# Two places instead of one for the copies of the linear attention's query and key projections

## The chip, the cores and the metric

The kernel runs on one core of one Trainium2 chip. The metric is the device time of one launch in microseconds (us), as the median of several runs. A core has five engines that run their own instruction streams: PE (matrix products; PEld is its loading of weights), DVE (vector), ACT (scalar functions and copies), POOL (a second vector engine) and SP, which here only issues transfers (DMAs). An engine takes its instructions in the order in which they were written; a semaphore makes it wait for another engine or for a DMA.

## The reference

One layer of a hybrid decoder on 16 learned meta tokens and 2048 tokens of width 1024, in float32:

```python
h = layer_norm(concat([meta, x]))
q_s, k_s, v_s, q_g, k_g, v_g, r_g, g_lr = split(h @ w_in + b_in)
o_s = sliding_window_gqa(q_s, k_s, v_s, sinks)        # 8 heads, window 128
log_g = log_sigmoid(g_lr @ w_gate_lr2 + b_gate_lr2) / 16
o_g = chunked_gla(q_g, k_g, v_g, log_g)               # linear attention, 4 heads
o_g = rms_norm(o_g, gla_norm_g) * silu(r_g)
h = layer_norm(ALPHA * h + concat([o_s, o_g]) @ w_out)
h = layer_norm(ALPHA * h + swiglu(h))                 # 1024 -> 2816 -> 1024
return h[16:]
```

The change concerns `q_g` and `k_g`, 256 columns each: four units of 128 columns of the input projection.

## The kernel before

The 2048 tokens are worked in four blocks `s` of 512. The program has three stages.

**First stage** (to about 400 us). Per block, the layer norm (`load_tokens`, 128 tokens at a time: load, normalise, transpose on PE, `tp`, split into a high and a low part `h`), the input projections for the window attention, the window attention itself, and the projections of `q_g` and `k_g`. A projection (`project`) is 24 PE matmuls of 512 columns (line 197, tile `pu`; three products of high and low parts over eight slices of the depth) into one of **two** PSUM buffers (`mm_psum`, `bufs=2`). An ACT instruction then adds the bias, writes the result to SBUF, and by that frees the PSUM buffer for the projection after the next. For `q_g` and `k_g` (`gla_qk`, lines 686 to 693) this copy is line 692, the tile is `gr`, and a DMA (line 693, on SP's queue, for the last block on ACT's) stores it to the scratch tensor `gqk_sc`, from where the second stage loads it. Units 6 to 9 are `gr` 0 to 3, unit 0 is the window's keys, unit 2 its first queries.

The window attention runs in steps of two 128-token blocks: scores (`s`, lines 627 and 628), mask and maximum on DVE, eight exponentials on ACT (line 643), sums, `pr` scaled on POOL (line 652), then a transpose of the meta part (`pmn` on ACT, `tm` on PE, `ptm`), transposes of the rest (`pt`, line 668), the high part `pch` (ACT) and low part `pcl` (DVE) of these, their masked forms `pbh` (DVE, line 672) and `pbl` (POOL, line 673), and the products with the values (`oa`, lines 675 and 680), whose copy `ms` is stored too.

**Second stage** (to about 930 us). Value, gate and output-gate projections, the chunked linear attention (`lp`, `amat`, `op`, `ot`), the output projection (`po`) with its residual (`yo`, line 930), layer norm and transposes (`nt`, line 943). **Third stage**: the feed-forward network, with a fast matrix scheme of seven products instead of eight.

The program names steps in the order of the string `WINDOW_STEPS` (`... V1 G3 S3 G2 G1 V2 ...`, where `G2` is `gla_qk` with `c = 2`), but this is not the order in which an engine gets them. `tile.TileContext(nc, schedule_with_timeline_sim=True)` lays the instructions of each engine out by a planner that follows the readiness of the tiles in a time model; only steps marked `held` keep the written order. A tile's count of places (`bufs`) therefore sets two things: what must wait at run time, and where the planner puts every later instruction. With `bufs=1`, the copy to `gr` can start only when the store of the previous `gr` has read it.

Of the kernel before, what the change touches and what calls it, by code (L numbers as in the profile page):

```python
# [8 lines left out]
F32 = mybir.dt.float32  # L9
# [5 lines left out]
P = 128  # L15
# [108 lines left out]
def body(ctx, tc, t, seq):  # L124
# [150 lines left out]
    with ExitStack() as c1:  # L275
# [3 lines left out]
        wp = c1.enter_context(tc.tile_pool(name="wp", bufs=1))  # L279
# [242 lines left out]
        def project(u, s, h, want_meta=False):  # L522
            w, pt = begun.pop((u, s), None) or (units_ahead.pop((u, s), None) or unit(t["w_u"][u], f"u{u}_{s}", P, None, key=u), mm_psum(f"pu{u}_{s}"))
            terms = lambda a, b: [m for k in range(KT) for m in ((w[:, 0, k, :], a(k)), (w[:, 0, k, :], b(k)), (w[:, 1, k, :], a(k)))]
            c = halves[1] if s == 0 and u < EARLY_UNITS else slice(0, TB)
            last_matmul[:] = [matmuls(pt[:, c], terms(lambda k: at(h, 0, k)[:, c], lambda k: at(h, 1, k)[:, c]), held if s == 0 and u < 2 else lambda i: i)]
            if s == 0 and u in FIRST_UNITS[:-1]:
                ahead(FIRST_UNITS[FIRST_UNITS.index(u) + 1], 0)
            if want_meta:
                metas[u] = w  # L530
            return pt
# [3 lines left out]
        def project_meta(o, u, b):  # L535
            w = metas.pop(u)
            pm = acc_psum(f"pm{u}")[:, : 2 * NM].rearrange("p (a m) -> p a m", m=NM)
            for k in range(KT):
                nc.tensor.matmul(pm, w[:, 0, k, :], hm[:, :, k, :], start=(k == 0), stop=False)
                nc.tensor.matmul(pm[:, 0, :], w[:, 1, k, :], hm[:, 0, k, :], start=False, stop=(k == KT - 1))  # L540
            nc.scalar.activation(o, pm[:, 0, :], AF.Identity, bias=b)
            nc.vector.tensor_tensor(o, o, pm[:, 1, :], op=ALU.add)
# [143 lines left out]
        def gla_qk(s, c, h):  # L686
            u = 6 + c
            pt = project(u, s, h, s == 0 and c >= 2)
            if s == 0 and c >= 2:
                project_meta(kTm[:, c - 2, :], u, bu[:, u : u + 1])  # L690
            raw = wp.tile([P, 512], F32, tag="gr", name=f"gr{s}_{c}", bufs=1)
            nc.scalar.activation(raw, pt, AF.Identity, bias=bu[:, u : u + 1])  # L692
            (nc.scalar if s == NSB - 1 else nc.sync).dma_start(gqk_sc[s * NB : (s + 1) * NB, :, c, :].rearrange("n p q -> p n q"), raw.rearrange("p (n q) -> p n q", q=P))

# [17 lines left out]
        for s in range(NSB):  # L712
            if s == NSB - 2:
                with behind(anchor):
                    tri, head, bvg, gng, eye, lev, w2, brh, brg = gla_constants()
            if s + 1 < NSB:
                hid[s + 1] = hidden(s + 1)
            for what in WINDOW_STEPS.split():
                op, k = what[0], int(what[1])
                if op == "q":  # L720
                    qs[s, k] = swa_q(s, k, hid[s])
                elif op == "S":
                    swa_scores(s, k, {c: qs.get((s, c)) for c in range(4)})
                elif op == "V":
                    swa_values(s, k)
                elif op == "G":
                    gla_qk(s, k, hid[s])
                elif s + 1 < NSB:
                    if op == "L":
                        with behind(ends if (s, k) == (0, 0) else ()):  # L730
                            load_tokens(s + 1, hid[s + 1], k)
                    elif op == "K":
                        (swa_keys, swa_vals)[k](s + 1, hid[s + 1])
                    else:
                        qs[s + 1, k] = swa_q(s + 1, k, hid[s + 1])
            if s == 0:
                with behind(stored_parts[-1:]):
                    for o, x in put_off:
                        nc.sync.dma_start(o, x)
# [105 lines left out]
    wp = c3.enter_context(tc.tile_pool(name="gw", bufs=1, reuse_waits="tile"))  # L845
# [490 lines left out]
    raw, factors = {}, {}  # L1336
# [258 lines left out]
    AFTER, f = {}, None  # L1595
    for what in FIRST_PRODUCTS.split():
        if what[0] == "P":
            f = EARLY[int(what[1])]
# [147 lines left out]
```

## Time and profile before

| | |
|---|---|
| median of 3 runs | 2222.5 us (2222.38 to 2226.02) |
| the profiled execution: its own time | 2216.87 us |
| its span, first to last instruction | 2215.0 us |
| PE busy | 2158.8 us, 97% of the span |
| mean granted PE clock | 0.993 |
| copies to `gr` (line 692) | 16, 687 ns each (median), 57.9 to 378.0 us |
| their stores to `gqk_sc` | 12 by SP, 4 by ACT; 256 KB each, 5.1 us to landing (median; 2.3 to 10.5) |

Time outside the span is 2216.87 - 2215.0 = 1.9 us. PE is busy nearly throughout, so what counts are the intervals in which PE waits, and the clock that it is granted. A group's row in the profile has, after the bar, its busy time, the mean of one instruction, and the idle time just before its instructions with what ended most of it. A row of the timeline has start, length, engine, line, operation, the number of instructions merged, and in brackets the idle time before the first and what ended it. PE's instructions overlap in the pipeline, so lengths of single matmuls are longer than their distance: a 512-column matmul follows another after about 0.23 us, a 128- or 256-column one after 0.12 us.

### The profile page before, as it was taken

To read this page: it belongs to the slowest core of one execution; us is meant where nothing else is said; L and a number is where in the kernel's file an instruction comes from. 1 tells how busy PE (TensorE), PEld (TensorE's weight loads), DVE (VectorE), ACT (ScalarE), POOL (GpSimd) and SP (SyncE) were. 2 spreads that over 40 slices of the span, in tenths; PEclk is the share of its full clock that TensorE was granted. 3 is DMA by queue.
4 is the path that set the end of the run, shared out by engine and by line. 5 is a ranking of instruction groups with operands and counts; after the bars stand their busy time and mean duration, and the time that the engine had idled before them with its cause. 6 is when DMAs were issued, how large, how long until landed. Compare 5 with 4: busy or idle time off the path is not lost.

```text
span 2215.0 us, 31559 instructions
## 1 busy us (share of the span) xinstructions
PE 2158.8 (97%) x11564; PEld 1858.7 (84%) x11564; DVE 1444.7 (65%) x2285; ACT 838.1 (38%) x1477; POOL 1220.2 (55%) x951
## 2 busy tenths in 40 slices
PE   8899999999999999999999999999999999999998
PEld 7788888889999998878888888788888888888886
DVE  6556645466745576368998567766656555876787
ACT  5544644544352443342223223322223242232443
POOL 4656645655634071368776666776666536432433
PEclk9999999999999999999999999999999999999999
DMA  8987773576786787766352318523232299655463
GB/s 296 316 277 252 254 268 127 193 277 226 290 294 225 253 310 244 274 252 219 130 196 103 131 45 286 189 101 109 90 125 81 98 360 330 219 185 177 166 232 124
DMA packets 181918, 460.92 MB, mean 208 GB/s; under 512 B 16978, under 2 KB 65011, under 8 KB 167684
## 3 DMA queue, kind: packets, MB, share of 16 engines
q1 hardware_dynamic: 176804, 452.26, 58.1%
q10 hardware_dynamic: 4960, 6.65, 0.8%
q8 instruction: 92, 1.51, 0.3%
q14 instruction: 62, 0.51, 0.1%
HBM read 306.67 MB, written 152.17 MB: 207 GB/s over the span
## 4 chain that ended last, share of the span: by engine, by line
PE 85%; DMA 4%; DVE 4%; POOL 3%; issue 2%; ACT 2%; SPq 0%; DVEq 0%; POOLq 0%; ACTq 0%
PE t L197 20%; PE d L1377 18%; PE b L197 14%; PE pu L197 13%; PE po L197 6%; PE pv L197 4%; PE lp L1151 2%; PE oa L680 1%; DMA r_t<-t_sc 1%; DMA cb<-n_scT 1%; DMA x<-x 1%; PE s L627 1%; PE s L628 1%; ACT pr L643 1%; PE nt L943 1%
## 5 line engine op out<-in xcount | busy, mean ns | idle before, releaser
L1377 PE MATMUL d<-B,A 128*128 128x512 f32 x1848 | 419.0, 389 | 0.0
L1377 PEld LDWEIGHTS d<-B,A 128*128 128x128 f32 x1848 | 346.9, 188 | 72.0
L197 PE MATMUL t<-h_t,ps 128*128 128x512 f32 x1584 | 367.9, 390 | 3.2 <-DMA ps<-parts_ps 2.4
L197 PEld LDWEIGHTS t<-h_t,ps 128*128 128x128 f32 x1584 | 296.8, 188 | 65.8 <-issue 2.1
L197 PE MATMUL pu<-h,hl_u 128*128 128x512 f32 (+1 forms) x1032 | 249.3, 389 | 7.2 <-ACT gr L692 4.5
L197 PE MATMUL b<-h_b,pa 128*128 128x512 f32 x1032 | 241.9, 390 | 0.3 <-ACT pa L185 0.2
L197 PEld LDWEIGHTS b<-h_b,pa 128*128 128x128 f32 x1032 | 193.7, 188 | 41.3 <-ACT pa L185 0.7
L186 POOL TENSOR_TENSOR pa<-a,pa 128x1024 fp32r<-128x1024 f32 x62 | 160.7, 2591 | 103.8 <-ACT pa L185 103.8
L197 PEld LDWEIGHTS pu<-h,hl_u 128*128 128x128 f32 x1032 | 184.0, 197 | 38.8 <-ACT gr L692 5.1
L197 PE MATMUL po<-hl_o,msh 128*128 128x256 f32 x1024 | 198.3, 289 | 4.8 <-DVE yo L930 3.1
L186 DVE TENSOR_TENSOR A<-rA,A 128x1024 fp32r<-128x1024 f32 (+1 forms) x78 | 117.2, 1527 | 119.7 <-ACT A L185 119.7
L197 PEld LDWEIGHTS po<-hl_o,msh 128*128 128x128 f32 x1024 | 162.1, 191 | 6.6 <-DVE yo L930 4.2
L185 ACT ACTIVATE A<-rA 128x1024 fp32r<-128x1024 f32 (+1 forms) x78 | 78.6, 1042 | 215.2 <-PE d L1377 200.2
L197 PE MATMUL po<-hl_o,msl 128*128 128x256 f32 x512 | 146.3, 286 | 0.0
L1647 DVE TENSOR_TENSOR u<-u,t 128x512 f32<-128x512 f32 x132 | 89.3, 680 | 84.2 <-PE t L197 84.1
L197 PE MATMUL b<-h_b,ps 128*128 128x512 f32 x528 | 126.9, 396 | 2.9 <-ACT h_b L185 2.8
L197 PE MATMUL t<-h_t,pa 128*128 128x512 f32 x528 | 123.8, 390 | 0.0
L1573 POOL TENSOR_TENSOR a<-a,a 128x1024 f32<-128x1024 f32 x42 | 121.2, 2887 | 1.6
L197 PEld LDWEIGHTS b<-h_b,ps 128*128 128x128 f32 x528 | 100.8, 191 | 25.0 <-ACT h_b L185 3.2
L197 PEld LDWEIGHTS t<-h_t,pa 128*128 128x128 f32 x528 | 99.0, 188 | 20.4
L185 ACT ACTIVATE ps<-a 128x1024 fp32r<-128x1024 f32 x63 | 66.7, 1059 | 123.4 <-PE t L197 81.9
L185 ACT ACTIVATE pa<-a 128x1024 fp32r<-128x1024 f32 x62 | 65.8, 1060 | 110.1 <-PE t L197 52.7
(355 smaller groups left out, 4292.0 us busy)
## 6 DMA issues: line engine op xcount, KB each, us to landing
hl_u<-w_u SPq DMA_DIRECT2D x42, 1024.0 KB, 6.7
a<-w_gu SPq DMA_DIRECT2D x84, 512.0 KB, 4.2
rA<-a_sc SPq DMA_DIRECT2D x66, 512.0 KB, 4.6
w<-w_d SPq DMA_DIRECT2D x50, 512.0 KB, 5.5
hl_o<-w_o SPq DMA_DIRECT2D x24, 1024.0 KB, 8.0
hT_sc<-h SPq DMA_DIRECT2D x32, 512.0 KB, 6.0
gh<-hT_sc SPq DMA_DIRECT2D x16, 1024.0 KB, 10.5
w_u<-hl_u SPq DMA_DIRECT2D x14, 1024.0 KB, 8.3
```

The lines of the kernel that those rows point to most:

```text
L185: hold(nc.scalar.activation(hi, src, AF.Copy))
L186: hold((lo_eng or nc.vector).tensor_tensor(lo, src, r32(hi), op=ALU.subtract))
L197: last = hold(nc.tensor.matmul(out, l, r, start=(i == 0), stop=(i == n - 1)))
L627: nc.tensor.matmul(sp[:, :272], q, khh[:, hh, w], start=True, stop=False)
L628: nc.tensor.matmul(sp[:, :272], q, kll[:, hh, w], start=False, stop=True)
L643: nc.scalar.activation(pr[:, n, x, :], pr[:, n, x, :], AF.Exp, bias=nm[:, n, x : x + 1], scale=SLOPES[c0 + x // 2 + 4 * (x % 2)], accum_ou ...
L680: nc.tensor.matmul(oa[:, n], l, m, start=False, stop=(hh == 1 and i == 5))
L943: nc.tensor.transpose(tp[:, n, :], self.ys[n][:, k * P : (k + 1) * P], ident)
L1151: nc.tensor.matmul(o[:, P * j : P * j + P], kl[:, j, :], x[:, :, j, :], start=True, stop=True)
L1377: nc.tensor.matmul(pt, a_[:, a, ca], fb[:, b, cb], start=(p == 0 and j == 0), stop=(p == NP - 1 and j == 2))
L1573: sub = lambda o, x, y: nc.gpsimd.tensor_tensor(o, x, y, op=ALU.subtract)
L1647: nc.vector.tensor_tensor(o[i], x[i], y[i], op=ALU.add)
```

## The change

The tile of the copies of `q_g` and `k_g` gets two places in SBUF:

```diff
@@ -688,7 +688,7 @@
             pt = project(u, s, h, s == 0 and c >= 2)
             if s == 0 and c >= 2:
                 project_meta(kTm[:, c - 2, :], u, bu[:, u : u + 1])
-            raw = wp.tile([P, 512], F32, tag="gr", name=f"gr{s}_{c}", bufs=1)
+            raw = wp.tile([P, 512], F32, tag="gr", name=f"gr{s}_{c}", bufs=2)
             nc.scalar.activation(raw, pt, AF.Identity, bias=bu[:, u : u + 1])
             (nc.scalar if s == NSB - 1 else nc.sync).dma_start(gqk_sc[...], raw...)
```

It takes 2 KB more of each partition in the pool `wp`, and no instruction is added or removed. But the planner now orders much of the program otherwise: from PE's row 149 (near 105 us) to its row 2626 (near 930 us) the rows stand in another order, and the other engines' likewise; behind that only a few rows of the second group of feed-forward products differ. Three places follow; a `+` is a row of the changed kernel, a `-` one of the kernel before; the last number of a name tells tiles of one name apart.

**First place: the first block's key unit 8.** On ACT, in the window attention's first steps; `gr_2` is the copy of unit 8, `h` and `x` belong to the layer norm:

```order
 L185 ACTIVATE h_0_712<-tp_0_1063 128x4x128
 L660 ACTIVATE pmn_0_846<-pr_0_784 128x128
+L692 ACTIVATE gr_2_1413<-pu_0_1362,bu 128x512
 L180 ACTIVATE x_1508<-x_1508,lm_in_1519,lr_in_1517 128x1024
 L185 ACTIVATE h_1_713<-tp_1_1070 128x4x128
```

The copy stood behind the eight exponentials of the second attention step; now it stands ahead of them. On PE, some instructions later, `pu_1_1547` is unit 0 of the next block (it takes the PSUM buffer that `gr_2`'s copy frees), `oa_0` the first step's products with the values:

```order
 L680 MATMUL oa_0_851<-pch_0_1_884,vl 128x256
+L197 MATMUL pu_1_1547<-h_0_712,hl_u_1_1545 128x512
 L680 MATMUL oa_0_851<-pcl_0_1_885,vh 128x256
 L391 MATMUL tp_1_1534<-ident,x_1508 128x128 x4
+L197 MATMUL pu_1_1547<-h_0_712,hl_u_1_1545 128x512 x11
 L680 MATMUL oa_0_851<-pbh_0_1_886,vdh 128x256
 L680 MATMUL oa_0_851<-pbh_0_1_886,vdl 128x256
```

The first twelve of unit 0's 24 matmuls now stand ahead of `oa<-pbh`; before, all of them stood behind the step's last `oa` and four scores. A little later on PE, the second attention step, in the kernel before:

```order
 L668 MATMUL pt_1_1_1215<-ident,pr_1_948 128x128 x4
 L197 MATMUL pu_1_1648<-h_0_712,hl_u_1_1646 128x512 x12
 L197 MATMUL pu_1_1648<-h_1_713,hl_u_1_1646 128x512 x4
 L627 MATMUL s_3_0_1151<-khh,qs_3_942 128x272
 L628 MATMUL s_3_0_1151<-kll,qs_3_942 128x272
 L680 MATMUL oa_1_1187<-pch_1_0_1193,vh 128x256
```

and in the changed one:

```order
 L668 MATMUL pt_1_1_1215<-ident,pr_1_948 128x128 x4
 L627 MATMUL s_2_1_1146<-khh,qs_2_1112 128x272
 L628 MATMUL s_2_1_1146<-kll,qs_2_1112 128x272
 L680 MATMUL oa_1_1187<-pch_1_0_1193,vh 128x256
 L680 MATMUL oa_1_1187<-pch_1_0_1193,vl 128x256
 L680 MATMUL oa_1_1187<-pcl_1_0_1194,vh 128x256
 L680 MATMUL oa_1_1187<-pbh_1_0_1195,vdh 128x256
```

Sixteen matmuls of unit 2 stood between the transposes `pt` and the products that need what is made of them; now two scores stand there, and unit 2 comes behind the products.

**Second place: PE in the second block**, near 205 us; `tm_1_2220` is the transpose of the meta part of that block's second attention step, `pu_2_2540` and `pu_2_2641` are units 0 and 2 of the third block:

```order
 L628 MATMUL s_3_1_2174<-kll,qs_3_1986 128x272
-L661 MATMUL tm_1_2220<-ident,pmn_1_2221 128x128
-L668 MATMUL pt_1_0_2227<-ident,pr_1_1992 128x128 x4
-L197 MATMUL pu_2_2540<-h_0_1766,hl_u_2_2538 128x512
-L197 MATMUL pu_2_2641<-h_0_1766,hl_u_2_2639 128x512
-L675 MATMUL oa_1_2226<-ptm_1_2224,vbd 128x128 x2
-L668 MATMUL pt_1_1_2254<-ident,pr_1_1992 128x128 x4
+L391 MATMUL tp_1_2527<-ident,x_2501 128x128 x4
+L197 MATMUL pu_2_2540<-h_0_1766,hl_u_2_2538 128x512 x11
+L197 MATMUL pu_2_2641<-h_0_1766,hl_u_2_2639 128x512 x10
 L627 MATMUL s_2_0_2180<-khh,qs_2_2151 128x272
```

In the changed kernel `tm` follows two rows below this piece, behind 21 matmuls of the projections; before, it followed the scores at once.

**Third place: PE at the end of the second stage**, near 905 us; `nt_7` is the last group of transposes of the third block's `yo` tiles, `po_1_1` and `po_2_1` are output products of the fourth block:

```order
 L197 MATMUL po_1_1_10306<-hl_o_1_1_10278,msl_9993 128x256
+L943 MATMUL nt_7_10268<-ident,yo_0_9266 128x128
+L943 MATMUL nt_7_10268<-ident,yo_1_9268 128x128
+L943 MATMUL nt_7_10268<-ident,yo_2_9270 128x128
+L943 MATMUL nt_7_10268<-ident,yo_3_9272 128x128
 L197 MATMUL po_1_1_10306<-hl_o_1_1_10278,msh_9992 128x256
-L943 MATMUL nt_5_10252<-ident,yo_0_9266 128x128
-L943 MATMUL nt_5_10252<-ident,yo_1_9268 128x128
-L943 MATMUL nt_5_10252<-ident,yo_2_9270 128x128
-L943 MATMUL nt_5_10252<-ident,yo_3_9272 128x128
 L197 MATMUL po_2_1_10332<-hl_o_1_0_10276,msh_9992 128x256
```

The last transposes stood behind the 24 matmuls of `po_2_1`; now they stand one matmul ahead of its first. The buffer of `yo_0` is the one into which the fourth block's last residual tile is loaded once they are done.

## The prediction

> **What bounds the kernel now.** I read the page first: engines, the chain that ended last, the costliest groups.
>
> ```profile
> PE 2158.8 (97%) x11564; PEld 1858.7 (84%) x11564; DVE 1444.7 (65%) x2285; ACT 838.1 (38%) x1477; POOL 1220.2 (55%) x951
> PE 85%; DMA 4%; DVE 4%; POOL 3%; issue 2%; ACT 2%; SPq 0%; DVEq 0%; POOLq 0%; ACTq 0%
> L197 PE MATMUL pu<-h,hl_u 128*128 128x512 f32 (+1 forms) x1032 | 249.3, 389 | 7.2 <-ACT gr L692 4.5
> ```
>
> PE is the bound, so a change is worth what it takes off PE's idle time or adds to its clock. Line 692 is the largest releaser of idle time that is named for a projection: 4.5 us. Next I read who waits for `gr`, and PE's timeline there.
>
> ```profile
>   PE pu L197: 4.5, 2
>   ACT gr L692: 2.9, 3
> ...
> 58.60 0.74 PE L197 MATMUL pu<-h,hl_u 128*128 128x512 f32 x2 [1.06 <-ACT gr L692]
> ...
> 106.60 0.39 PE L680 MATMUL oa<-pbh,vdh 128*128 128x256 f32 x1 [0.66 <-DVE pbh L672]
> 111.86 6.03 PE L197 MATMUL pu<-h,hl_u 128*128 128x512 f32 x19 [3.41 <-ACT gr L692]
> ```
>
> The 4.5 us are two waits. That at 58.60 lies ahead of the first row that is moved (near 105 us) and stays. The one at 111.86 is 3.41 us: unit 0 needs the PSUM buffer that the copy of unit 8 frees. SP and ACT show why the copy came so late:
>
> ```profile
> 100.61 1.49 SPq L693 DMA_DIRECT2D gqk_sc<-gr  x1
> ...
> 107.36 0.42 ACT L643 ACTIVATE pr<-pr,nm 128x144 f32<-128x144 f32 x1 [0.78 <-DVE nm L639]
> ...
> 111.13 0.67 ACT L692 ACTIVATE gr<-pu,bu 128x512 f32<-128x512 f32 x1
> 114.10 0.31 ACT L660 ACTIVATE pmn<-pr 128x128 f32<-128x128 f32 x1 [2.29 <-POOL pr L652]
> ```
>
> It is queued behind exponentials that run without a gap from 107.36 to 111.13. The planner put it there because the one place was still being stored: the store of the `gr` before was issued by SP at 100.61 only. Two windows behind the wait, and the whole stretch that is reordered:
>
> ```profile
> 112.00:114.00 2.00, 2.00 (x5) 1.61 (x6) 1.76 (x6) 0.00 (x0) 2.00 (x2) 0.50 1.12 365
> 114.00:116.00 2.00, 2.00 (x8) 1.57 (x8) 0.21 (x1) 1.46 (x2) 0.57 (x2) 0.77 1.03 391
> ...
> 100.00:400.00 300.00, 291.04 (x1748) 256.78 (x1746) 171.89 (x548) 151.81 (x416) 167.09 (x143) 0.99 0.69 229
> 400.00:930.00 530.00, 513.09 (x3755) 480.31 (x3755) 312.86 (x678) 219.85 (x480) 241.09 (x401) 1.00 0.74 267
> ```
>
> (Columns: window, its length, PE, PEld, DVE, ACT, POOL busy, granted clock, DMA share, GB/s.) PE idles 8.96 + 16.91 = 25.9 us between 100 and 930 us. That is all that any new order can win there, apart from the clock.
>
> **The change part by part.** No instruction is added, so each term is a wait that goes, comes or moves. I go through the places in time.
>
> *The wait itself:* **-3.41 us**. In the new order the copy stands among ACT's work near 94 us, before the exponentials, and its own PSUM tile was finished before that. Unit 0's first half can then start once `h` is there: its low part is done at 104.49 + 0.68 = 105.17,
>
> ```profile
> 104.49 0.68 DVE L186 TENSOR_TENSOR h<-tp,h 128x512 fp32r<-128x512 f32 x1
> ```
>
> and PE arrives at the first of the twelve at about 105.1, needing only the high part for it. What hides the copy's wait is now 5.6 us of unit 0 (24 matmuls, 0.235 apart: the row of sixteen at 121.38 below, less a last one of 0.39, over 15). Were `h` later, PE would stand on `h` instead. Range: 0 to -3.41.
>
> *The clock behind it:* half speed for 2 us and 0.77 for 2 us cost 2 x 0.50 + 2 x 0.23 = **-1.46 us**, if no idle stretch of that kind remains. [...]
>
> *The 0.66 us for `pbh`* at 106.60 are covered by the eleven matmuls now ahead of it (11 x 0.235 = 2.6): **-0.66**.
>
> *New: the second attention step has lost its cover.* Sixteen projection matmuls (3.74 us) stood between its `pt` and its `oa`. How long the chain takes is in its rows of before:
>
> ```profile
> 119.47 0.60 PE L668 MATMUL pt<-ident,pr 128*128 128x128 f32 x4
> 121.38 3.91 PE L197 MATMUL pu<-h,hl_u 128*128 128x512 f32 x16
> ...
> 121.39 0.69 DVE L186 TENSOR_TENSOR pcl<-pt,pch 128x512 fp32r<-128x512 f32 x1
> 122.00 1.41 DVE L672 TENSOR_TENSOR pbh<-pch,mprev 128x512 fp32r<-128x512 f32 x1
> 122.81 1.75 POOL L673 TENSOR_TENSOR pbl<-pcl,mprev 128x512 fp32r<-128x512 f32 x1
> ```
>
> The first four transposes take four distances of 0.12 and end near 119.95; `pbh` is ready 3.46 us later, `pbl` 4.61. In the new order PE wants `pbh` after 13 short matmuls (13 x 0.12 = 1.6) and `pbl` 0.5 later. So PE waits some 1.9 for the one and 0.6 for the other: **+2.5 us**. Low end 0 (DVE did a step of scores ahead of `pcl` here; without it the chain is some 1 us shorter, and a later PE would hide the rest). High end: the second half's `pbl`, for which POOL needs 1.75 more, waits 0.5 too, and the clock's 1.46 is lost again: 4.5. I take the rows as they stand.
>
> *New: `tm` of that step.* Its `pmn` was ready at 114.41 and PE came later, being held up. Now PE has 24 projection matmuls, nine `oa` and eight scores from 105.1 on, some 8.3 us with the transposes, and stands at `tm` near 113.4. ACT gains one copy there, since `ms` moves behind the exponentials, but unit 0's copy (`kr`) now stands ahead of `pmn`, each about the 0.67 of `gr`; so `pmn` ends near 114.2: **+0.8** (0 to 1.4). POOL, which scales `pr`, is free there.
>
> *Queues that the store is moved past.* SP issues the store of unit 8 earlier, ahead of a load of `x`, two stores of the layer norm and the load of unit 2's weights:
>
> ```profile
> 109.37 1.33 SPq L221 DMA_DIRECT2D hl_u<-w_u x1
> ...
> hl_u<-w_u SPq DMA_DIRECT2D x42, 1024.0 KB, 6.7
> ```
>
> An issue takes 1.3 to 1.5 us here (the rows at 109.37 and 100.61), so these weights land at about 109.4 + 1.5 + 6.7 = 117.6; unit 2 starts near 119: **0**, and the cover is 1.4 us. If it were gone (SP's queue another 3 us late), a wait of 1.6 us would stand there.
>
> *Near 205 us* PE waits for `pmn`, which stood behind a copy that waited for its single place:
>
> ```profile
> 204.30 0.69 ACT L692 ACTIVATE gr<-pu,bu 128x512 f32<-128x512 f32 x1 [0.29 <-DMA gqk_sc<-gr]
> 204.89 0.30 ACT L660 ACTIVATE pmn<-pr 128x128 f32<-128x128 f32 x1
> 205.24 0.33 PE L661 MATMUL tm<-ident,pmn 128*128 128x128 f32 x1 [1.30 <-ACT pmn L660]
> ```
>
> With 21 projection matmuls (4.9 us) ahead of `tm` this goes: **-1.30** (0 to -1.30).
>
> *Near 915 us* PE waits for a residual add that waits for a load into a buffer that the last `nt` frees:
>
> ```profile
> 908.48 0.60 PE L943 MATMUL nt<-ident,yo 128*128 128x128 f32 x4
> ...
> 914.43 0.75 DVE L930 SCALAR_TENSOR_TENSOR yo<-yo,po 128x256 f32<-128x256 f32 x2 [1.36 <-DMA yo<-h_sc]
> 914.90 0.38 PE L197 MATMUL po<-hl_o,msh 128*128 128x256 f32 x1 [2.61 <-DVE yo L930]
> ```
>
> `nt_7` moves ahead of 25 matmuls of 0.12 us, 3.0 us in all, which would cover the 2.61. SP's queue must follow, and more stores stand around that load; I take **-2.0** (0 to -2.61).
>
> *All other waits between 115 and 930 us* are dealt anew: 25.9 - 4.07 - 1.30 - 2.61 = 17.9 us in some thirty waits of under 2 us. The attention chains of the later steps stand no closer in the new order than before, and some that were short have more between `pt` and `oa`. I expect the same total: **0**, with half of it either way, -9 to +9.
>
> Sum: -3.41 - 1.46 - 0.66 + 2.5 + 0.8 - 1.30 - 2.0 + 0 = **-5.5 us**; the profiled execution would go from 2216.87 to 2211.4. The runs' median is 2222.5, 5.6 above that execution, so I set the forecast against the median: 2222.5 - 5.5 = **2217.0 us**. Its own range: without the gains at 205 and 915 us, -2.2; with a third of the other waits gone, -11: 2211.5 to 2220.3.
>
> **The rivals.**
>
> *A new wait takes the old one's place* (no change). The second step's chain waits with 4.5 in place of 2.5, `tm` with 1.4, and the places at 205 and 915 us give nothing: -5.53 + 4.5 + 1.4 = +0.4, 2222.9 us. For it: the cover of 16 matmuls is gone, by the order. [...]
>
> *The new order costs more than the wait* (slower). The mechanism is PE's clock: somewhere in the reordered 800 us, PE stands for about 2.5 us and then runs at half speed. This trace prices it by the worst such place, at 58 to 72 us:
>
> ```profile
> 60.76 1.12 PE L391 MATMUL tp<-ident,x 128*128 128x128 f32 x4 [1.42 <-DVE h L186]
> ...
> 60.00:70.00 10.00, 8.77 (x32) 7.78 (x33) 9.43 (x16) 2.03 (x7) 9.25 (x6) 0.52 0.84 274
> ```
>
> 1.06 + 1.42 us of waiting, then 10 x 0.48 = 4.8 us of clock: 7.3 us. Two such places less the sum above: -5.5 + 14.6 = +9.1, 2231.6 us; it decides from new waits of 10 us on. For it: 2598 lines of difference on PE, from a planner that does not know the clock. Against it: the 2.61 us at 914.90 went without a loss (1.00 in the window 400 to 930).
>
> *The copy moves and PE gains nothing, since the copy is still held up on ACT:* 2222.5. Against it: nothing but PE's own result is waited for in front of it. This is part of the no-change case.
>
> **How the numbers follow.** The forecast has 0.58, no change 0.26, slower 0.16. A measurement of this kernel tells about 0.2%, 4.4 us, from no change; of the forecast's 0.58 I count 0.08 below that. So faster 0.50, same 0.34, slower 0.16. The range reaches from 2209 (0.06 below) to 2227 (0.10 above, most of the slower case); the likeliest case's own is above.
>
> **What would show it.** Right: no wait of `pu` for `gr` after 100 us, clock 1.00 from 105 to 120 us, waits of `oa` on `pbh` and `pbl` near 117 us of 1 to 3 us, no wait for `pmn` above 1 us near 200 us, and no wait for `yo` above 1 us before 930 us; behind 1000 us every wait as before, some 5 us earlier. Wrong: granted clock under 1.00 anywhere between 105 and 930 us, PE idle there above 25.9 us, or a wait of the second step above 4 us.

## The result, and the profile after

| | before | after |
|---|---|---|
| median | 2222.5 us (5 runs, 2217.15 to 2226.02) | **2238.1 us** (5 runs, 2232.41 to 2240.98) |
| ratio, 95% interval | | **1.0073** (1.006 to 1.0087): slower |
| profiled execution, its span | 2216.87, 2215.0 us | 2232.41, 2230.5 us |
| mean granted PE clock in it | 0.993 | 0.988 |

The forecast was 2217.0 us, in a range of 2209 to 2227. The change costs 15.6 us.

The page of after, in the rows that answer to those shown of before (engines, the projections' group):

```profile
PE 2166.1 (97%) x11564; PEld 1864.1 (84%) x11564; DVE 1434.8 (64%) x2285; ACT 837.1 (38%) x1477; POOL 1218.8 (55%) x951
L197 PE MATMUL pu<-h,hl_u 128*128 128x512 f32 (+1 forms) x1032 | 248.3, 388 | 7.5 <-ACT h L185 2.9
```

The same instructions keep PE busy 7.3 us longer (2158.8 before), at a mean granted clock of 0.988 in place of 0.993, and PE idles 2230.5 - 2166.1 = 64.4 us in place of 56.2. The largest releaser of the projections is no longer `gr` but `h`.

**The first place came out as forecast.** ACT's and PE's timeline of after:

```profile
94.30 0.69 ACT L692 ACTIVATE gr<-pu,bu 128x512 f32<-128x512 f32 x1 [0.55 <-PE pu L197]
...
105.50 0.40 PE L197 MATMUL pu<-h,hl_u 128*128 128x512 f32 x1
106.21 2.75 PE L197 MATMUL pu<-h,hl_u 128*128 128x512 f32 x11
114.40 0.33 PE L661 MATMUL tm<-ident,pmn 128*128 128x128 f32 x1 [0.60 <-ACT pmn L660]
117.16 0.39 PE L680 MATMUL oa<-pcl,vh 128*128 128x256 f32 x1 [0.32 <-DVE pcl L186]
```

and its window there (columns as below):

```profile
110.00:120.00 10.00, 8.68 (x54) 7.15 (x53) 7.39 (x31) 4.69 (x14) 4.38 (x4) 1.00 1.05 330
```

The copy of unit 8 is done at 95.0, unit 0 starts at 105.50 without a wait for `gr`, the clock is 1.00, and the second attention step waits a little on `tm` and `oa`.

**The loss lies in the second stage.** Windows of before and of after by stage (window, its length, then PE, PEld, DVE, ACT, POOL busy with their counts, granted clock, DMA share, GB/s). Before:

```profile
400.00:510.00 110.00, 103.36 (x693) 91.25 (x693) 64.60 (x148) 51.54 (x121) 65.94 (x107) 1.00 0.69 248
510.00:685.00 175.00, 175.00 (x1272) 165.06 (x1271) 100.71 (x213) 77.19 (x158) 87.23 (x149) 1.00 0.80 290
685.00:940.00 255.00, 244.73 (x1869) 233.66 (x1868) 154.81 (x337) 95.91 (x207) 90.72 (x150) 1.00 0.70 253
```

After:

```profile
100.00:400.00 300.00, 292.54 (x1743) 257.78 (x1741) 166.90 (x542) 152.47 (x415) 166.53 (x141) 0.99 0.70 229
400.00:510.00 110.00, 105.48 (x702) 94.45 (x702) 68.19 (x154) 51.46 (x124) 67.46 (x109) 0.97 0.70 252
510.00:685.00 175.00, 168.43 (x1174) 157.59 (x1173) 95.02 (x203) 76.30 (x155) 85.93 (x144) 0.97 0.72 260
685.00:940.00 255.00, 243.72 (x1847) 232.50 (x1846) 146.48 (x326) 88.71 (x201) 87.09 (x149) 0.99 0.74 268
```

Before, PE does not idle at all from 510 to 685 us: 175.00 of 175.00, at full clock. After, it idles 6.57 us there, has a clock of 0.97, and gets 1174 matmuls done in place of 1272. The waits that PE has between 510 and 935 us say of what kind this is (releaser: us in total, times, the longest). Before, 9.9 us in all, of which the longest are:

```profile
PE po L197 <- DVE yo L930: 3.1, 2, 2.6
PE lp L1151 <- DVE amat L1153: 1.8, 1, 1.8
PE po L197 <- DMA hl_o<-w_o: 1.5, 1, 1.5
PE ot L1190 <- ACT ogn L1187: 1.2, 1, 1.2
```

After, 17.7 us, among them:

```profile
PE lp L1151 <- DVE xq L1146: 4.4, 5, 1.5
PE pu L197 <- DMA hl_u<-w_u: 2.9, 2, 2.1
PE po L197 <- ACT p L1655: 2.3, 1, 2.3
...
PE nt L943 <- ACT yo L180: 1.5, 1, 1.5
PE kt L1163 <- DVE e L1130: 1.3, 1, 1.3
```

Nearly every wait is another one. None has to do with `gr`.

Since no instruction is added, the two programs can be compared point by point: where both orders have issued the same set of PE instructions, how much later does the next one start than before? (One profiled execution each; in the first 60 us two executions of the same order differ by up to 3.4 us and have come together to 0.8 by 71.)

| start before, us | 71.5 | 115.9 | 131.6 | 508.7 | 621.9 | 683.2 | 914.9 | 2112.7 |
|---|---|---|---|---|---|---|---|---|
| after, us later | 0.0 | -5.7 | -3.3 | 0.1 | 8.1 | 12.0 | 15.3 | 15.9 |

The gain is there (-5.7, of which the second attention step takes 2.4 back), is lost between 131 and 508 us, and from 508 to 915 us another 15 us go. Between 131 and 508 us it is the clock that takes the gain: from 130 to 510 us PE idles 10.7 us, in place of 11.5 before, but the granted clock is 0.51 from 202 to 209 us, 0.58 from 400 to 404 and 0.57 from 461 to 465, where before has 1.00.

### The profile page after: what moved, and what is told of

The parts are those of the page before. It is cut to its first block, busy times and chain, and to the rows that moved or that the text cites. A ratio compares the mean times of both kernels' runs of the same rounds, so it can differ in the third digit from the quotient of the medians.

```text
span 2230.5 us, 31549 instructions
## 1 busy us (share of the span) xinstructions
PE 2166.1 (97%) x11564; PEld 1864.1 (84%) x11564; DVE 1434.8 (64%) x2285; ACT 837.1 (38%) x1477; POOL 1218.8 (55%) x951
## 4 chain that ended last, share of the span: by engine, by line
PE 86%; DVE 5%; DMA 4%; POOL 2%; issue 2%; ACT 1%; SPq 0%; DVEq 0%; ACTq 0%; POOLq 0%
PE t L197 21%; PE d L1377 17%; PE b L197 15%; PE pu L197 12%; PE po L197 7%; PE pv L197 4%; PE oa L680 2%; PE lp L1151 2%; PE s L627 1%; DMA hl_u<-w_u 1%; PE s L628 1%; PE nt L943 1%; PE oa L675 1%; DMA cb<-n_scT 1%; PE pt L668 1%
## 5 line engine op out<-in xcount | busy, mean ns | idle before, releaser
L185 ACT ACTIVATE ps<-a 128x1024 fp32r<-128x1024 f32 x63 | 66.6, 1058 | 115.9 <-PE t L197 74.8
L186 DVE TENSOR_TENSOR ps<-a,ps 128x1024 fp32r<-128x1024 f32 x42 | 75.9, 1807 | 50.5 <-ACT ps L185 50.5
```

The source lines that it names most:

```text
L185: hold(nc.scalar.activation(hi, src, AF.Copy))
L186: hold((lo_eng or nc.vector).tensor_tensor(lo, src, r32(hi), op=ALU.subtract))
```

## The experiments

Two things changed at once, the place and the order. My theory was now that the whole loss is the redrawn order. The rivals: that the second place costs by itself, that the loss begins with the moved copy and is carried on, and, in the words of the prediction, that it is the clock.

To part them, the order is held by hand. The program is planned once with one place and once with two, each plan is read as a list for each engine, and a third build is made in which each instruction is tied behind its predecessor in the wanted list, without a semaphore. The list may follow one plan up to a certain PE instruction and the other from there on:

```python
for k in order:
    e = engine[k]
    if e in last:
        tc.add_manual_dep(written[k], written[last[e]].name, ...NoSync..., reason="order")
    last[e] = k
```

`PLACES` is what stands as `bufs` in line 691; `PARTS` lists (plan with so many places, up to which PE instruction). All runs are timed beside runs of the kernel before on the same chip.

### Place and order apart

The order of before with two places:

```diff
+PLACES = 2
+PARTS = [(1, None)]
```

> Two places as in the change, but every instruction on every engine held to the order of the kernel before. Theory (the redrawn order is the whole loss, a second place by itself costs nothing): 2222.5 us, within 0.2% of before, half-clock stretches as before (33.6 us in sum). Rival (the second place itself costs, by its address, its semaphores or what its earlier stores collide with): 2238 us, a ratio near 1.007.

Measured: 2220.85 us, ratio 0.9999 (0.9987 to 1.001). The new order with one place:

```diff
+PLACES = 1
+PARTS = [(2, None)]
```

> One place as before, but every instruction held to the order that the change gets. Theory (order is the loss): 2238 us or more; the copy of unit 8 now waits near 94 us on ScalarE for the one place, which the store issued near 100 us frees, so 3 to 8 us more in the first stage: 2238 to 2246. Rival (the second place itself costs): back to about 2222 to 2230 us.

Measured: 2248.79 us, 1.0124 (1.0108 to 1.014). ACT's and PE's rows of this run show the wait, which is longer than I had put it:

```profile
105.31 0.69 ACT L692 ACTIVATE gr<-pu,bu 128x512 f32<-128x512 f32 x1 [12.71 <-DMA gqk_sc<-gr]
...
107.83 1.22 PE L675 MATMUL oa<-ptm,vbd 128*128 128x128 f32 x4 [7.23 <-ACT ptm L663]
```

With one place ACT stands 12.71 us on the store, and PE 7.23. So the second place itself costs nothing that can be measured, and the new order needs it; the order is the loss.

### Where the loss is

The old order up to 508 us, then the new one, and the mirror of this:

```diff
+PARTS = [(1, 2707), (2, None)]
```

> Two places, the order of before up to TensorE's instruction 2707 (508 us in both traces), then the order of the change. Theory (the loss lies behind 508 us, where the same instruction starts 0.05 us later than before at 508, 8.1 at 622, 12.0 at 683, 15.2 at 930): 2238 us, ratio about 1.007, and the half-clock stretch near 560 us there again. Rival (the loss begins with the moved copy and is only carried): 2222 us.

Measured: 2233.47 us, 1.0061 (1.0046 to 1.0076).

```diff
+PARTS = [(2, 2707), (1, None)]
```

> Two places, the order of the change up to TensorE's instruction 2707 (508 us), then the order of before: the mirror of the run with the halves the other way round. Theory (the two halves add up; the change as a whole is 1.0073, its second half alone 1.0061, so 0.0012 is left for the first half, most of it a granted clock that is lower by about 10 us of half speed at 202, 400 and 461 us while the waits are 2 us fewer): 2221 to 2226 us, ratio 1.000 to 1.002. Rival (the first half sets up a state, such as buffers or loads that come late, from which the loss behind 508 us follows): over 2230 us.

Measured: 2220.62 us, 0.9999 (0.9989 to 1.0009). Within the intervals the loss is all behind 508 us, and the first half does not set it up. The first of the two runs also shows what the clock has to do with it. Its window from 510 to 685 us, and its longest waits between 510 and 935 us:

```profile
510.00:685.00 175.00, 166.73 (x1191) 155.82 (x1191) 98.55 (x207) 76.82 (x157) 86.43 (x146) 1.00 0.75 266
```

```profile
PE lp L1151 <- DVE xq L1146: 4.4, 5, 1.5
PE pu L197 <- DMA hl_u<-w_u: 2.6, 1, 2.6
PE po L197 <- ACT p L1655: 2.5, 1, 2.5
PE kt L1163 <- DVE e L1130: 2.4, 1, 2.4
PE lp L1159 <- DVE amat L1157: 1.7, 2, 0.9
```

From 510 to 685 us the clock is 1.00 here, as before the change, and yet PE idles 8.27 us; over 510 to 935 us the waits are 20.7 us in place of 9.9. The mean granted clock of its six runs is 0.991, that of the 23 runs of before beside them 0.9915; the five runs of the change have 0.988. An estimate of time at full clock (mean time by mean clock) gives 2202.6 for before, 2215.3 for this run and 2211.0 for the change: here 12.7 us of the 13.5 are waits, in the change about 8 are waits and 7 or 8 clock. The end is nearly the same; why, no run shows. So the loss does not need the clock: the order of the second stage costs 13 us at the clock of before. In the change itself, though, about half of the loss is clock.

Two stretches of the new order alone, 508 to 622 us and from 683 us on:

```diff
+PARTS = [(1, 2707), (2, 3444), (1, None)]
```

> Two places, the order of the change for TensorE's instructions 2707 to 3444 alone (508 to 622 us), the order of before ahead of and behind them. Theory (the loss is a sum of waits, place by place; this stretch lost 5.9 us in the run that went over at 508 us, by five waits for xq and amat of 5.1 us in sum): 2225 to 2227 us, ratio 1.002 to 1.003, and the waits near 557 and 560 us again. Rival (a limit behind them takes such waits up later): 2220 to 2222 us, ratio under 1.001.

Measured: 2227.72 us, 1.0029 (1.0018 to 1.0041), with the waits where they were (1.16 us at 558.58, and PE's row behind it):

```profile
561.45 0.71 PE L1151 MATMUL lp<-xq,e 128*128 128x128 f32 x4 [1.48 <-DVE xq L1146]
```

```diff
+PARTS = [(1, 3832), (2, None)]
```

> Two places, the order of before up to TensorE's instruction 3832 (683 us), then the order of the change. Theory (sum of waits: 9.5 us of the 14 were lost ahead of 683 us, 4 to 6 us behind it, at 798, 896 and 899 us and behind 985 us): 2223 to 2226 us, ratio 1.0015 to 1.0027. Rival (the waits behind 683 us follow from the lateness that the stretch before brought): 2219 to 2221 us, ratio within 0.0005 of 1.

Measured: 2226.62 us, 1.0026 (1.0015 to 1.0037), with 1.53 us before `nt` at 888.37 and this before `po`:

```profile
891.67 0.58 PE L197 MATMUL po<-hl_o,msh 128*128 128x256 f32 x1 [2.86 <-ACT p L1655]
```

The two stretches add up to 0.0055 of the 0.0061; the rest is within the intervals, and the piece between them, 622 to 683 us, was not run alone. Each of the two stretches costs its time whatever comes ahead of it, and nothing behind it gives that back.

### What the removed wait is worth

The new order only through the first place, to 116 us and to 131 us:

```diff
+PARTS = [(2, 508), (1, None)]
```

> Two places, the order of the change for TensorE's first 508 instructions (to unit 0's first half, 110 us), then the order of before. Theory (the wait that the change removes is worth what the first place showed, 4.8 us from 71 to 110 us, and the rest of the redraw is what costs): 2217.5 us, ratio 0.9975 to 0.9985, with no wait of pu for gr over 1 us and no half clock at 111 us. Rival (the gain is given back at the next common wait whatever the order): 2222 us.

Measured: 2219.83 us, 0.9994 (0.9983 to 1.0006): this cannot be told from no change, and the theory's 0.9975 to 0.9985 is missed. This version moves unit 0's first half ahead but keeps the old order behind it, and there PE waits for the scores' maximum (below), with a clock of 0.72 from 120 to 130 us behind it:

```profile
117.12 0.36 PE L627 MATMUL s<-khh,qs 128*128 128x272 f32 x1 [1.66 <-DVE mx L630]
```

```diff
+PARTS = [(2, 601), (1, None)]
```

> Two places, the order of the change up to TensorE's instruction 601 (131 us, behind the second attention step), then the order of before. Theory (the removed wait and its neighbours are a real gain of 3.2 us at that point, which the order of before keeps to the end): 2218 us, ratio 0.998 to 0.999. Rival (the clock or a later wait takes it back, as when the order went back at 116 us, where half speed came 7 us later and for 6.8 us): 2221 to 2222 us, ratio 0.9995 to 1.0005.

Measured: **2217.5 us, 0.9988 (0.998 to 0.9997)**. This version has the second place, the gain at the first place and the old second stage, and it is faster than both kernels, though than the one before by a narrow margin: the interval ends at 0.9997. From 100 to 130 us its clock is 1.00 throughout, and its window from 510 to 685 us has no idle again:

```profile
510.00:685.00 175.00, 175.00 (x1274) 165.32 (x1273) 99.51 (x212) 76.70 (x157) 87.74 (x150) 1.00 0.80 291
```

### Can the waits be taken away one by one?

On the run that goes over to the new order at 508 us, three instructions or groups are moved within their engine's list (engine, first, behind the last, to before):

```diff
+MOVES = [("SP", 294, 295, 287), ("PE", 4517, 4519, 4529), ("DVE", 1201, 1202, 1200)]
```

> As the run that goes over to the order of the change at 508 us (2233.5 us, ratio 1.0061), with three places of its second half mended by hand: the load of unit 12's weights issued ahead of two loads and a store that it stood behind (wait of 2.60 us at 668 us), the two transposes of kt put behind ten matmuls of unit 12 that need nothing new (wait of 2.40 us at 798 us), and the last mixing product on VectorE put ahead of one subtraction (wait of 2.45 us at 899.5 us, 1.1 us of it). Theory (the loss is the sum of waits that the new order happens to have): the three give back 4 to 6 us, 2228 to 2230 us, ratio 1.0035 to 1.0045, and the first two waits are under 0.3 us in the trace. Rival (the loss sits in one limit behind the waits, such as VectorE or the loads, so a wait that is taken away comes back at the next place): 2232 to 2235 us, ratio 1.0055 to 1.007.

Measured: 2235.82 us, 1.0068 (1.0054 to 1.0082), so my theory failed here and the rival held. Its timeline, PE and SP:

```profile
675.74 7.34 PE L197 MATMUL pu<-gh,hl_u 128*128 128x512 f32 x24 [2.02 <-DMA hl_u<-w_u]
...
800.46 2.52 PE L197 MATMUL pu<-gh,hl_u 128*128 128x512 f32 x10 [1.69 <-DMA hl_u<-w_u]
...
659.12 0.32 SPq L221 DMA_DIRECT2D hl_u<-w_u  x1
...
664.04 0.32 SPq L221 DMA_DIRECT2D hl_u<-w_u  x1
```

and what SP waited for between 650 and 666 us:

```profile
SPq L221 <- PE pv L197: 8.3, 1, 8.3
```

The wait of 2.60 us for unit 12's weights is gone, but unit 13's come 2.02 us late. The load that I moved ahead is not held up by the queue: it overwrites a buffer that matmuls of `pv` still read, and SP stood 8.3 us on them, with everything behind it, unit 13's load among it (issued at 664.04, and at 659.2 without the move). The wait of 2.40 for `kt` is gone too, and the projection put ahead of it waits 1.69 for its own weights. The product put ahead on DVE gave nothing (2.71 us at 902.82 in place of 2.45). So the new order has `pv` close ahead of the projection whose weights take its buffer, and an earlier place in the queue did not mend that. The three moves together gave nothing back; whether others would, no run shows.

The other direction: SP's queue alone in the new order behind 508 us, the four engines in the old one.

```diff
+PARTS = [(1, 2707), (2, None)]
+OLD = ["PE", "DVE", "Activation", "Pool"]
```

> Two places; TensorE, VectorE, ScalarE and GpSimd keep the order of before all through, and SyncE's queue alone has the order of the change behind TensorE's instruction 2707 (508 us). Theory (the loss comes from how the instructions of TensorE and VectorE stand to each other; a load goes out when the buffer that it overwrites has been read, in either queue order): 2219 to 2224 us, ratio 0.999 to 1.002. Rival (the queue's order holds the weight loads back, as the wait of 2.60 us at 668 us and its successor at 675 us suggest): 2226 us or more, ratio over 1.003, with waits of pu for hl_u.

Measured: 2298.66 us, 1.0345 (1.0325 to 1.0364). The theory failed. The rival's bound is met, but neither expectation came near the size. Between 500 and 1020 us PE waits 9.4 us for `hl_u`, as the rival said, and up to 14.3 us at one place (`po` for `yo`). SP's own waits there show why:

```profile
SPq L952 <- ACT ntr L950: 46.4, 15, 9.3
SPq L1101 <- DVE amat L1157: 45.3, 5, 11.5
```

SP stands in order on stores (line 952) whose data, and on loads (line 1101) whose buffers, come at another time in the engines' old order, and the transfers behind them are late. So this run cannot say how much of the loss the queue's order makes in its own setting; it says that SP's list and those of the engines belong together. No run swaps the list of another single engine.

### Another change into the same order

Last, a change that has nothing to do with `gr`: one more place for the input tiles of the layer norm.

```diff
-            xt = wp.tile([P, D], F32, tag="xl", name=f"x_{r}", bufs=2)
+            xt = wp.tile([P, D], F32, tag="xl", name=f"x_{r}", bufs=3)
```

> Another change altogether: the copies of the projections keep their one place, and the input tiles xl get three places in place of two. The planner's order is a third one in the first stage, and behind 508 us it is, but for a few rows, the order that the two places for the copies got. Theory (the order of the second stage is what costs, whoever draws it): 12 to 15 us are lost behind 508 us again; with a first stage within 4 us of before either way, 2229 to 2239 us, ratio 1.0035 to 1.0085, with the waits for xq near 557 and 560 us and for p near 899 us. Rival (the second place of the copies does it): 2217 to 2225 us, ratio within 0.002 of 1.

Measured: 2240.33 us, 1.0086 (1.0068 to 1.0103), just above the expected range, with the same waits:

```profile
564.54 0.71 PE L1151 MATMUL lp<-xq,gqk 128*128 128x128 f32 x4 [1.16 <-DVE xq L1146]
567.41 1.22 PE L1151 MATMUL lp<-xq,e 128*128 128x128 f32 x4 [1.48 <-DVE xq L1146]
...
677.26 5.80 PE L197 MATMUL pu<-gh,hl_u 128*128 128x512 f32 x24 [2.84 <-DMA hl_u<-w_u]
...
808.13 0.44 PE L1163 MATMUL kt<-ident,e 128*128 128x128 f32 x2 [2.42 <-DVE e L1130]
```

This execution, the slowest of its six (2245.51 us), also lost time ahead of 508 us: there it is 9.7 us behind the profiled execution of the next run, which has the same lists up to that point. It begins with a product on DVE, the first of the two in its row, that took 8.25 us in place of 0.80 (more on it at the end), and PE stood 4.00 us for what came behind it:

```profile
430.31 8.59 DVE L1129 TENSOR_TENSOR e<-e,gqk 128x256 f32<-128x256 f32 x2 [2.99 <-ACT e L1125]
...
439.31 5.43 PE L197 MATMUL pv<-hl_vg,gh 128*128 128x272 f32 x24 [4.00 <-DVE vg L1036]
```

The same change with the old order from 508 us on:

```diff
+PARTS = [(3, 2707), (2, None)]     # plans with three and two places for xl
```

> Three places for the input tiles, one for the copies; the planner's order for that up to TensorE's instruction 2707 (508 us), then the order of before. Theory: the loss behind 508 us goes, so 12 to 15 us less than the same change with its own order: 2217 to 2225 us, ratio 0.998 to 1.002. Rival (the first stage of this order costs too, or sets up the loss): 2228 us or more.

Measured: 2223.44 us, 1.0017 (1.0005 to 1.0028). The second stage's order costs 0.0069 here, 0.0061 in the run with two places for `gr`: it is a loss of that order, whoever draws it, though executions differ by chance waits such as the one above, and the last digits are not firm. (This first stage itself costs some 0.0017.)

## Why the prediction was wrong

*The wait itself, the clock behind it, `pbh`, the second step, `tm`* (-3.41 - 1.46 - 0.66 + 2.5 + 0.8 = -2.23): **right** in sum, a little on the careful side. Up to 131 us the change is 3.3 us ahead, the version with only this part 3.7 (from -0.45 at 71 us to -4.17), and its runs gain 0.0012, 2.7 us. The removed wait, its clock and `pbh` (-5.53) came as forecast, -5.7. The second step gave back 2.4 of its 3.3, but not by the waits that I had named: PE's waits there are 0.60 us for `pmn`, 0.32 for `pcl`, 0.21 for `pbh` and 0.17 for the scores' maximum, 1.3 in all, where 1.9 for `pbh`, 0.6 for `pbl` and 0.8 for `pmn` were expected. The other 1.1 us stand in no wait that the profile shows, so that this term came near is partly luck.

*Near 205 us* (-1.30): the wait of `tm` for `pmn` did go, but PE now reaches the projection ahead of it before its `h` is there, and this is the rival "a new wait takes the old one's place", at a place where I had not looked. PE's row of after, and the window with half speed there:

```profile
203.35 1.22 PE L197 MATMUL pu<-h,hl_u 128*128 128x512 f32 x2 [2.40 <-ACT h L185]
```

```profile
202.00:209.00 7.00, 5.65 (x18) 4.83 (x19) 5.31 (x17) 3.71 (x10) 4.48 (x4) 0.51 0.77 216
```

*Near 915 us* (-2.0): the wait of 2.61 went, leaving three of 0.51, and is outweighed by waits of 1.53 and 2.34 us at 897 and 900 us. What was a gain at the named row was a loss in its stretch.

*All other waits dealt anew* (0, -9 to +9): **this is the step that failed**. From 131 us on the profiled execution loses 15.5 + 3.3 = 18.8 us, where -3.3 (205 and 915 us) and this 0 were expected; behind 508 us alone it is 13 us by the runs. The sum also put the clock behind the new waits at nothing. In the profiled execution of the change the clock is the larger part: from 130 to 940 us PE idles 28.5 us in place of 21.8, but the granted clock is 0.51 to 0.59 in six windows (202 to 209, 400 to 404, 461 to 465, 560 to 567, 645 to 649 and 898 to 905 us), where before has 1.00 throughout. What the clock lacks in these windows is 15 us, an estimate from their rows, some 13 of it while PE was busy. The run with the old order to 508 us shows that the waits alone can cost nearly as much. I had let the total of 17.9 us of waits be drawn again with the same mean. But those waits were not spread over the stretch: the row of before from 510 to 685 us, 175.00 busy of 175.00 at clock 1.00, shows no wait to win in 175 us. There a new order can hardly be better, only as good or worse, and it was worse by 6.6 us of idle time, with the clock lower as well, or by 8.3 us at full clock. My bounds should have been lopsided, with the idle time of each stage as the most that it can give and no such limit on the other side. (The lower end of the likeliest case also has a slip: with a third of the 17.9 us gone the sum is -11.5, not -11.)

*The rival "the new order costs more than the wait"* (0.16, 2231.6 us) was what happened, and its sign and size were near. Half speed is there in the change, in the six windows; five of them have idle time of PE in them (0.38 us from 400 to 404 to 1.82 us from 898 to 905) and one, 645 to 649 us, has none: that half speed answers idle stretches, as the rival has it, is not shown. The loss does not need it either, as the run with the old order to 508 us loses 13 us at the clock of before, so the nearness of the size is partly luck. My sentences on what would show me wrong did their work: the clock is under 1.00 in 400 to 510 and 510 to 685 us, and PE idles 7.46 us from 100 to 400 and, by the three rows behind it, 22.4 to 940 us, 29.8 in all.

What stays open is whether one limit stands behind these waits. A stretch of the order costs by itself, mending three waits moved two of them on, with late weights behind both, and SP's list mixed with the others' says nothing on it; for the waits for `xq` at 557 to 572 us, where a load has no part, no run took them away.

## What to carry to other kernels

Where a planner sets the order, a change to one tile's places is two changes, and the second, the new order of everything behind it, can be the larger: hold the order by hand and measure the place and the order apart. Before forecasting a redraw, read PE's idle time stage by stage; a stage without any can hardly win, and the sum of idle time is, apart from the clock, an upper bound of the gain, not a spread about zero. When a redraw loses, keep the piece of the new order that holds the gain and the old order behind it; here that took the kernel from 1.0073 to 0.9988 (0.998 to 0.9997).

## What the runs showed of the hardware

**A product of VectorE (DVE) took longer where it met one of GpSimd (POOL).** It stands behind one of the waits for `xq`. In the run with the old order to 508 us, on POOL, DVE and PE:

```profile
557.94 2.35 POOL L186 TENSOR_TENSOR hl_o<-st_o,hl_o 128x1024 fp32r<-128x1024 f32 x1 [1.99 <-ACT hl_o L185]
...
557.28 0.42 DVE L1146 TENSOR_TENSOR xq<-e,gqh 128x256 f32<-128x256 f32 x1
558.50 2.07 DVE L1146 TENSOR_TENSOR xq<-e,gqh 128x256 f32<-128x256 f32 x1 [0.46 <-PE lp L1151]
...
560.62 0.71 PE L1151 MATMUL lp<-xq,e 128*128 128x128 f32 x4 [1.48 <-DVE xq L1146]
```

The same product takes 0.42 us at 557.28 and 2.07 us when it is issued 0.56 us into a product of GpSimd; it ends at 560.57, 0.28 behind GpSimd's at 560.29. In the kernel before, the two meet at a later moment of GpSimd's product:

```profile
556.14 2.37 POOL L186 TENSOR_TENSOR hl_o<-st_o,hl_o 128x1024 fp32r<-128x1024 f32 x1 [10.34 <-DVE xq L1146]
...
557.84 0.94 DVE L1146 TENSOR_TENSOR xq<-e,gqh 128x256 f32<-128x256 f32 x1 [0.26 <-PE lp L1151]
```

Here `xq` came 1.70 us into GpSimd's product, took 0.94 and ended at 558.78, 0.27 behind it (558.51). PE waited 1.48 us for the product in the one order and did not idle in the other (175.00 of 175.00 from 510 to 685 us). Not every instruction of VectorE took longer there: in the kernel before, 1.02 us into the same product of GpSimd, an add to `yo` took 0.42 us:

```profile
557.16 0.42 DVE L930 SCALAR_TENSOR_TENSOR yo<-yo,po 128x256 f32<-128x256 f32 x1
```

What parts the two, no run shows.

Once there was more than one product of GpSimd. In the run with three places for the input tiles, the first of DVE's two products at 430.31 (its row stands above) was issued 0.30 us into a GpSimd product and ended at 438.56, 0.28 behind the last of 21 GpSimd products that followed each other without a gap (438.28). In the run after it the same product was issued at 428.28, in the midst of the same GpSimd products, and took 0.80 us; in after it was issued at 431.62 and 435.99, among such GpSimd products too, and took 0.69 and 0.72 us. So one such product lasted to the end of the train and the others did not; what decides it, no run shows.

**Half speed did not follow the length of a wait.** In the run with the old order to 508 us, PE's waits of 2.60 and 2.40 us, in its list above, left the clock at 1.00, as its windows behind them show, while in after the wait of 2.40 us ahead of 203.35 goes with 0.51 from 202 to 209 us (both rows stand above):

```profile
668.00:672.00 4.00, 4.00 (x18) 3.33 (x19) 0.82 (x2) 0.00 (x0) 4.00 (x10) 1.00 1.02 420
800.00:804.00 4.00, 4.00 (x21) 3.33 (x20) 1.82 (x4) 1.68 (x4) 4.00 (x11) 1.00 1.03 411
```

In after, the clock was 0.59 in a window in which PE is busy all the time, as it is in the three microseconds ahead (3.00 of 3.00 from 642 to 645 us, at clock 1.00), mostly with matmuls of 128 columns or few rows:

```profile
645.00:649.00 4.00, 4.00 (x16) 3.29 (x17) 0.95 (x2) 2.67 (x6) 0.00 (x0) 0.59 0.82 241
```

In the clock's records in the traces of before and after, the stretches at half speed are 3.41 us long or two or three times that, but for the last of each (9.81 and 9.97 us): in order of time 3.41, 10.24, 3.41 and 6.83 us in before, and 10.24, 6.83, 3.41, 3.41, 6.83, 3.41, 6.83 and 3.41 us in after. What brings half speed on, and what sets these lengths, no run here shows: a wait of 2.40 us went with it at one place and not at another, and the clock fell near 645 us without a wait.
